# A hybrid-attention layer on one core: sums of output weights formed by DMA in another stage, head outputs loaded one product earlier

## The chip, the cores and the metric

The kernel runs on one core of a Trainium2 chip. Such a core has TensorE (PE, matrix products), VectorE (DVE), ScalarE (ACT) and GpSimd (POOL), and SyncE (SP), which here only starts transfers. Each engine has one queue of instructions and works it off in order; semaphores hold an instruction until what it needs is there. Transfers between the chip's memory and the core's on-chip memory run on 16 DMA engines, which the queues of SP, ACT and POOL feed. The metric is the device time of one execution, in microseconds (us).

## The reference: what is computed

One layer on a sequence of 512 tokens with 16 learned tokens ahead of it, model width 2048, all in 32-bit floats. In short:

```python
u    = rms_norm(h, pre_w)
q_a, ckv, z_a, iq, ik, iw, q_b, k_b, v_b, z_b, g_a, g_b = split(u @ w_in)
# A: index scores pick 128 keys per query; 8 heads attend over a 256-wide latent
o_a  = sparse_attention(q_a, rms_norm(ckv), topk(index(iq, ik, iw)))
# B: 8 heads, difference of two softmaxes, then an RMS norm per head
o_b  = rms_norm((softmax(q1 k1 + bias) - lam * softmax(q2 k2 + bias)) @ v_b) * (1 - lam_init)
y_a  = (o_a * silu(z_a)) @ w_o_a
y_b  = (o_b * silu(z_b)) @ w_o_b
mix  = sigmoid(g_a) * y_a + sigmoid(g_b) * y_b
h    = h + rms_norm(mix @ w_out, post_w)
```

## The kernel before

Every large product is made of three 16-bit products: a float is split into a high and a low 16-bit half after scaling by a power of two. So each block of weights goes the same way. SP loads two halves of 512 KB (tile `raw`, L187 in branch B, L1148 in the gate stage). ACT squares them (`junk`, L123). POOL takes the largest sum over all rows (`rows`, L128). VectorE makes a power of two of it (`exp`, `scale`, L135 to L140). ACT writes the high half (`hi` or `wh`, L169), VectorE the low half (`lo` or `wl`, L170), and PE multiplies both (L289 to L291, L1015). A `raw` buffer is free for the next load when the low half is written.

The stages, by the profiled execution: norm and first projections (to about 100 us), index scores (to 175), branch B (175 to 575), branch A with its query projections (575 to 784), the gates (784 to 1224), the two output projections `w_o` (to 1394) and the product with `w_out` (to the end).

*Branch B* (loop over 8 heads at L882): for each head the projections of q, k and v, each called a unit, of two weight halves. Between the halves the attention of the head before is worked off in steps (`step()`): scores L738 and L739, exponentials L668, their difference `pr` L744, its transposes L675 and the product with V. K is copied out of PE's accumulator by ACT and VectorE at L784 and L785, V by ACT at L900. The bias rows `G` are loaded by SP at L656, and a head's result is stored at L749 and L756.

*Sums of output weights.* The product with `w_out` uses Strassen's scheme, 7 block products in place of 8, and needs four sums of blocks of `w_out`. A chain (`wt_chain`, L254) makes them for one part of 256 KB: two loads by SP (L265) into tiles `wt`; accumulating transfers by POOL's queue (L263), which add another block of memory to the tile; and four stores by SP to a scratch array `wout_t` (L260). There are 16 chains, so 32 loads, 64 additions and 64 stores. A chain goes in six steps with a `yield` between, and later additions wait for the stores of what the tile held before. Before the change two chains belong to each head and advance one step at each `between()` (L878), six times a head, in tiles of the pool `opool`.

*The gates* (`Run`, L1039): the products with the columns of z and g are taken in pairs of blocks, again by Strassen's scheme with 7 products a pair (`Pair.mm`, L1002). Each product is 24 matmuls. `Run.run` walks the list of 154 products, n = 0 to 153, in an order with fixed leads: loads of a pair (blocks A22, A12, A11, A21), squares, scale, sums of the blocks S1 to S4 (L1126) and their split are called so many products ahead. At product 2 of a pair `con.tiles()` took two result tiles and, for pairs of z, called `load_o` for the two heads: it loads a head's output `o` (L1093) and, for branch B's heads, the row factors `rb` (L1096), and multiplies them (L1098). When a pair ends, `gate_o` multiplies by the gate (L1105, L1107) and the result is stored (L1109). The merge gates g store theirs through ACT's queue.

The order on each queue is program order, but for a planner that places the calls; loads, additions and stores of the chains carry `keep_in_program_order`, which holds them in the order of the code against each other.

Of the kernel before, what the change touches and what calls it, by code (L numbers as in the profile page):

```python
# [20 lines left out]
P = 128  # L21
# [6 lines left out]
NH = 8  # L28
# [40 lines left out]
def layer_kernel(ctx, tc, xt_d, xn_d, cols_d, w0_d, wi_d, wkv_d, wo_d, wout_d, lam_d, post_d,  # L69
# [184 lines left out]
    def wt_chain(k, n, tags):  # L254

        t = [opool.tile(HB, F32, tag=tag, name="wt") for tag in tags]
        q = [[wout_d[ci, di, k, :, 512 * n:512 * n + 512] for di in range(2)] for ci in range(2)]

        def put(i, x):
            tc.keep_in_program_order(nc.sync.dma_start(tscr[i][k, :, 512 * n:512 * n + 512], x))  # L260

        def add(x, src):
            tc.keep_in_program_order(nc.gpsimd.dma_start(x, src, accum_op=ALU.add))  # L263
        for i in range(2):
            tc.keep_in_program_order(nc.sync.dma_start(t[i], q[0][i]))  # L265
        yield
        add(t[0], q[0][1])
        add(t[1], q[1][1])
        yield
        put(0, t[0])  # L270
        put(2, t[1])
        yield
        add(t[1], q[0][0])
        yield
        put(1, t[1])
        yield
        add(t[1], q[1][0])
        yield
        put(3, t[1])

    wt_now = []

    def wt_step():
        for g in list(wt_now):
            if next(g, "end") == "end":
                wt_now.remove(g)
# [144 lines left out]
    def side0():  # L431
# [11 lines left out]
        sqi = SC[3][:, :(NB + 1) * 64].rearrange("p (a b) -> p a b", b=64)  # L443
# [30 lines left out]

    def bias_rows():
        oh = [SC[2 + t][:32, :NF // 2] for t in range(2)]
        rb = SC[1][:32, :NIH]
        nc.scalar.dma_start(rb, rb_d)
        pf = lgt()
        for t in range(2):  # L480
            nc.scalar.dma_start(oh[t], oh_d[:, t * NF // 2:(t + 1) * NF // 2])
            nc.tensor.matmul(pf[:NIH, t, :NF // 2], rb, oh[t], start=True, stop=True)
        fsb = pp.tile([NIH, NF], F32, name="fsb")
        nc.vector.tensor_copy(split2(fsb), pf[:NIH, :, :NF // 2])
        nc.scalar.dma_start(fscr.ap(), fsb)
# [16 lines left out]

    piq = [psum(), psum()]
# [374 lines left out]
    def between():  # L878
        wt_step()
        run_topk(TK.pop(0))  # L880

    for h in range(NH):  # L882
        for i in range(2):
            wt_now.append(wt_chain(h, i, [f"o{6 + 4 * (h % 2) + 2 * i + x}" for x in range(2)]))
# [51 lines left out]
    for h in range(NH):  # L936
# [3 lines left out]
        for acc, un in proj_q("qa", h):  # L940
            step()
            wt_step()
# [33 lines left out]
    class Pair:  # L976
# [25 lines left out]
        def mm(self, i):  # L1002
# [14 lines left out]
            v = self.v  # L1017
            if i in (1, 5, 6):
# [20 lines left out]
    class Run:  # L1039
# [23 lines left out]
        def run(self, hooks=None):  # L1063
# [3 lines left out]
            for n, (x, i) in enumerate(self.todo):  # L1067
# [3 lines left out]
                for f in (hooks or {}).get(n - len(self.todo), ()):  # L1071
                    f()
                self.pairs[x].mm(i)

    ogpool = ctx.enter_context(tc.tile_pool(name="ogpool", bufs=1, reuse_waits="tile"))
    zg = ExitStack()
# [14 lines left out]
    def load_o(i):  # L1091
        o = wide("o")
        nc.sync.dma_start(o, oscr[i])  # L1093
        if i >= NH:
            r = wide("rb")
            nc.sync.dma_start(r, bass.AP(tensor=rsq.tensor, offset=rsq.offset + (i - NH) * 512,  # L1096
                                         ap=[[0, P], [1, 512]]))
            nc.vector.tensor_mul(o, o, r)  # L1098
        return o
# [3 lines left out]
    def gate_o(i, o, sz):  # L1103
        if i < NH:
            nc.vector.tensor_mul(sz, sz, o)  # L1105
        else:
            nc.vector.scalar_tensor_tensor(sz, o, gsub, sz, op0=ALU.mult, op1=ALU.mult)  # L1107
# [44 lines left out]
    class Gate:  # L1152
        def __init__(self, func, end, begin=None):
            self.func, self.begin, self.end = func, begin, lambda x: end(x, self)

        def tiles(self):
            self.r = wide("r0"), wide("r1")
            if self.begin is not None:
                self.o = self.begin()
# [341 lines left out]
```

## Time and profile before

| what | before |
|---|---|
| time, median of 3 runs (lowest, highest) | 1552.25 us (1551.74, 1559.52) |
| time of the profiled execution | 1555.86 us |
| its span in the profile | 1554.1 us |
| mean granted clock of TensorE | 0.973 of full |
| busy: PE, VectorE, ACT, POOL | 1438.2, 1104.7, 978.3, 144.3 us |
| moved by DMA | 257.27 MB, 166 GB/s in the mean |
| PE busy in branch B (175 to 575) | 351.4 of 400 us |
| PE busy in the gates (784 to 1224) | 412.3 of 440 us |

A wait in the profile stands for the idle time of an engine ahead of an instruction, with what released it: "PE acc L675 <- DVE pr L744" is PE, idle until VectorE had written the softmax difference. An idle engine costs time only if it ends up delaying PE. Nearly all of the span PE is busy, so what counts is where PE stands still, and where its granted clock is at the lower of its two levels, 1.2 instead of 2.4 GHz.

### The profile page before, as it was taken

The numbers are of one execution on the slowest core, as the hardware profiler recorded it, in microseconds if no ns is written. First come the engines' busy times: TensorE is split into PE (matmuls) and PEld (weight loads), VectorE is DVE, ScalarE is ACT, GpSimd is POOL, SyncE is SP. The second block draws the span as 40 slices with busy tenths as digits, with TensorE's granted clock in tenths as the row PEclk, the third lists the DMA queues.
The fourth block names the chain that finished last, engine by engine and source line by source line (L and its number), as shares of the span: only waits on it lengthen the run. The fifth ranks groups of instructions, "written<-read, shape, count | busy, mean of one in ns | idle before, by whom it ended". The sixth has DMA issues, their size and how long they took to land. (4 is left out here: it accounts for less than half of the span.)

```text
span 1554.1 us, 25269 instructions
## 1 busy us (share of the span) xinstructions
PE 1438.2 (93%) x9475; PEld 1079.5 (69%) x9475; DVE 1104.7 (71%) x2091; ACT 978.3 (63%) x1735; POOL 144.3 (9%) x199
## 2 busy tenths in 40 slices
PE   7799977989898989999999989999999899999997
PEld 7678755766675766665578878888888444458885
DVE  7875756566666677776578887777778455566788
ACT  6365555666565577677677787777778444436555
POOL 3500121212111100000000000000000001000001
PEclk9999998999899999999999999999999999999999
DMA  6383487787777744321545544444344554446774
GB/s 208 124 278 95 126 236 177 202 223 197 180 203 177 210 123 123 116 85 60 191 132 186 178 137 140 144 139 147 122 139 163 174 158 149 150 160 233 240 249 148
DMA packets 104218, 257.27 MB, mean 166 GB/s; under 512 B 12072, under 2 KB 16392, under 8 KB 103968
## 3 DMA queue, kind: packets, MB, share of 16 engines
q1 hardware_dynamic: 86224, 223.86, 44.9%
q0 software_dynamic: 9216, 16.78, 7.0%
q10 hardware_dynamic: 8656, 15.02, 2.7%
q8 instruction: 74, 1.21, 0.3%
q14 instruction: 48, 0.39, 0.1%
HBM read 211.42 MB, written 47.41 MB: 167 GB/s over the span
## 5 line engine op out<-in xcount | busy, mean ns | idle before, releaser
L123 ACT ACTIVATE junk<-raw 128x1024 bf16<-128x1024 f32 x192 | 201.9, 1052 | 139.1 <-DMA raw<-in_wi_dram 122.4
L1015 PEld LDWEIGHTS <-wh 128*128 128x128 f16 x2464 | 242.2, 98 | 61.4 <-issue 32.2
L289 PE MATMUL acc<-u,hi 128*128 128x264 f16 (+1 forms) x832 | 267.8, 322 | 1.0 <-DVE va L836 0.5
L291 PE MATMUL acc<-u,lo 128*128 128x264 f16 (+1 forms) x832 | 266.4, 320 | 1.1 <-DVE lo L170 1.1
L290 PE MATMUL acc<-u,hi 128*128 128x264 f16 (+1 forms) x832 | 266.7, 321 | 0.0
L1015 PE MATMUL acc<-tu,wh 128*128 128x256 f16 x1408 | 237.5, 275 | 27.5 <-DVE r L1024 15.9
L1015 PE MATMUL acc<-tu,wl 128*128 128x256 f16 x704 | 193.7, 275 | 0.0
L169 ACT ACTIVATE hi<-raw,scale 128x1024 f16<-128x1024 f32 x104 | 118.9, 1145 | 116.4 <-PE acc L290 115.1
L1015 PE MATMUL acc<-u,wh 128*128 128x256 f16 x1056 | 175.3, 273 | 0.3 <-ACT q L1019 0.3
L289 PEld LDWEIGHTS <-hi 128*128 128x128 f16 x1088 | 108.2, 99 | 80.6 <-issue 6.0
L291 PEld LDWEIGHTS <-lo 128*128 128x128 f16 x1088 | 108.0, 99 | 78.7 <-DVE lo L170 1.8
L170 DVE SCALAR_TENSOR_TENSOR lo<-raw,scale,hi 128x1024 f16<-128x1024 f32 x104 | 132.7, 1279 | 41.1 <-ACT hi L169 40.6
L290 PEld LDWEIGHTS <-hi 128*128 128x128 f16 x1088 | 108.2, 99 | 73.8 <-issue 1.1
L170 DVE SCALAR_TENSOR_TENSOR wl<-S,scale,wh 128x1024 f16<-128x1024 f32 x88 | 112.7, 1282 | 55.1 <-ACT wh L169 55.0
L128 POOL PARTITION_ALL_REDUCE rows<-ssq x90 | 47.4, 527 | 1066.9 <-ACT junk L123 960.5
L1015 PE MATMUL acc<-u,wl 128*128 128x256 f16 x528 | 143.9, 273 | 0.0
L1015 PEld LDWEIGHTS <-wl 128*128 128x128 f16 x1232 | 121.1, 98 | 14.8
L169 ACT ACTIVATE wh<-S,scale 128x1024 f16<-128x1024 f32 x88 | 100.3, 1141 | 32.1 <-DVE S L1126 32.1
L289 PE MATMUL acc<-og,hi 128*128 128x512 f16 x256 | 97.0, 379 | 0.0
L290 PE MATMUL acc<-og,hi 128*128 128x512 f16 x256 | 97.0, 379 | 0.0
L291 PE MATMUL acc<-og,lo 128*128 128x512 f16 x256 | 97.0, 379 | 0.0
L170 DVE SCALAR_TENSOR_TENSOR wl<-raw,scale,wh 128x1024 f16<-128x1024 f32 x66 | 84.3, 1278 | 10.0 <-ACT wh L169 9.9
(313 smaller groups left out, 2908.1 us busy)
## 6 DMA issues: line engine op xcount, KB each, us to landing
raw<-in_wi_dram SPq DMA_DIRECT2D x172, 512.0 KB, 4.7
wt<-in_wout_dram POOLq DMA_DIRECT2D x64, 256.0 KB, 5.4
wout_t<-wt SPq DMA_DIRECT2D x64, 256.0 KB, 5.1
raw<-in_wo_dram SPq DMA_DIRECT2D x32, 512.0 KB, 3.8
raw<-wout_t SPq DMA_DIRECT2D x32, 512.0 KB, 4.8
raw<-in_wout_dram SPq DMA_DIRECT2D x24, 512.0 KB, 5.6
wt<-in_wout_dram SPq DMA_DIRECT2D x32, 256.0 KB, 5.1
sg<-r ACTq DMA_DIRECT2D x32, 256.0 KB, 2.9
```

The lines of the kernel that those rows point to most:

```text
L123: nc.scalar.activation(j, src, AF.Square, accum_out=dst)
L128: nc.gpsimd.partition_all_reduce(r, ssq, P, bass_isa.ReduceOp.max)
L169: nc.scalar.activation(hi, src, AF.Copy, scale=s)
L170: nc.vector.scalar_tensor_tensor(lo, src, s, hi, op0=ALU.mult, op1=ALU.subtract)
L289: nc.tensor.matmul(out, aH, bH, start=start, stop=False)
L290: nc.tensor.matmul(out, aH, bL, start=False, stop=False)
L291: nc.tensor.matmul(out, aL, bH, start=False, stop=stop)
L1015: nc.tensor.matmul(acc, a[:, k, :], b, start=first and k == 0 and x == 0, stop=last and x == 2, skip_group_check=True)
```

## The change

It has three parts. The chains of weight sums leave branch B and the query loop of branch A and run in the gates: at every odd product n, `wt_step` advances two of them, in two fixed pairs of tiles (og12 to og15 of the pool `ogpool`), and starts the next two when both are through. A chain then takes seven steps, so that 16 chains in two slots take 56 odd products, n = 1 to about 112. Second, a gate pair of z takes its head outputs and row factors at product 1 instead of product 2, in tiles of `ogpool` of their own, and the multiplication of the two moves from the load to the pair's end. Third, the one-hot rows and the bias table are loaded ahead of the loop over the index queries, and the squares of the index keys use a tile of the preparation pool.

```diff
--- before.py
+++ after.py
@@ -253,7 +253,7 @@
 
     def wt_chain(k, n, tags):
 
-        t = [opool.tile(HB, F32, tag=tag, name="wt") for tag in tags]
+        t = [state["ogpool"].tile(HB, F32, tag=tag, name="wt") for tag in tags]
         q = [[wout_d[ci, di, k, :, 512 * n:512 * n + 512] for di in range(2)] for ci in range(2)]
 
         def put(i, x):
@@ -278,12 +278,15 @@
         yield
         put(3, t[1])
 
-    wt_now = []
+    wt_todo = [(k, n) for k in range(8) for n in range(2)]
+    wt_now = [None, None]
 
     def wt_step():
-        for g in list(wt_now):
-            if next(g, "end") == "end":
-                wt_now.remove(g)
+        for x in range(2):
+            if wt_now[x] is None and wt_todo:
+                wt_now[x] = wt_chain(*wt_todo.pop(0), [f"og{12 + 2 * x + y}" for y in range(2)])
+            if wt_now[x] is not None and next(wt_now[x], "end") == "end":
+                wt_now[x] = None
 
     def mm3(out, aH, aL, bH, bL, start, stop):
         nc.tensor.matmul(out, aH, bH, start=start, stop=False)
@@ -440,7 +443,7 @@
         nc.vector.tensor_reduce(st, ikn, AX.X, ALU.add)
         nc.vector.tensor_scalar(st, st, 1.0 / 64, None, op0=ALU.mult)
         nc.vector.tensor_tensor(ikn, ikn, stb, ALU.subtract)
-        sqi = SC[3][:, :(NB + 1) * 64].rearrange("p (a b) -> p a b", b=64)
+        sqi = pp.tile([P, T], F32, tag="sq", name="sqi", bufs=3)[:, :(NB + 1) * 64].rearrange("p (a b) -> p a b", b=64)
         nc.vector.tensor_mul(sqi, ikn, ikn)
         nc.vector.tensor_reduce(st, sqi, AX.X, ALU.add)
         rstd_cols(st, st, 64)
@@ -472,13 +475,17 @@
             nc.scalar.copy(ckH[r], ckv[r])
             nc.vector.tensor_sub(ckL[r], ckv[r], f32(ckH[r]))
 
+    oh = [SC[2 + t][:32, :NF // 2] for t in range(2)]
+    rb = SC[1][:32, :NIH]
+
+    def bias_loads():
+        nc.scalar.dma_start(rb, rb_d)
+        for t in range(2):
+            nc.scalar.dma_start(oh[t], oh_d[:, t * NF // 2:(t + 1) * NF // 2])
+
     def bias_rows():
-        oh = [SC[2 + t][:32, :NF // 2] for t in range(2)]
-        rb = SC[1][:32, :NIH]
-        nc.scalar.dma_start(rb, rb_d)
         pf = lgt()
         for t in range(2):
-            nc.scalar.dma_start(oh[t], oh_d[:, t * NF // 2:(t + 1) * NF // 2])
             nc.tensor.matmul(pf[:NIH, t, :NF // 2], rb, oh[t], start=True, stop=True)
         fsb = pp.tile([NIH, NF], F32, name="fsb")
         nc.vector.tensor_copy(split2(fsb), pf[:NIH, :, :NF // 2])
@@ -500,6 +507,7 @@
         uH[k], uL[k] = u[:, 0], u[:, 1]
         split16(uH[k], uL[k], xT[k], gs[:, k:k + 1])
 
+    bias_loads()
     piq = [psum(), psum()]
     nxt = [first_weights(kp, 3 * P, 5 * P) for kp in range(2)]
     for kp in range(KT // 2):
@@ -876,12 +884,9 @@
                 pending.pop(0)()
 
     def between():
-        wt_step()
         run_topk(TK.pop(0))
 
     for h in range(NH):
-        for i in range(2):
-            wt_now.append(wt_chain(h, i, [f"o{6 + 4 * (h % 2) + 2 * i + x}" for x in range(2)]))
         for acc, un in proj_q("qb", h):
             step(2 if len(pending) == 7 else 1)
             between()
@@ -939,7 +944,6 @@
         step(len(pending) - 2)
         for acc, un in proj_q("qa", h):
             step()
-            wt_step()
         una = wpool.tile([P, 1], F32, tag="una", name="una", bufs=2)
         nc.vector.tensor_scalar(una, un, A_SCALE, None, op0=ALU.mult)
         qh = ap_.tile([P, 512], F32R, tag="q", name="qh", bufs=4)
@@ -1015,6 +1019,8 @@
                     nc.tensor.matmul(acc, a[:, k, :], b, start=first and k == 0 and x == 0,
                                      stop=last and x == 2, skip_group_check=True)
             v = self.v
+            if i == 1:
+                self.con.early()
             if i in (1, 5, 6):
                 nc.scalar.copy(self.q(i), acc)
             elif i == 2:
@@ -1070,9 +1076,12 @@
                 self.prep(n + self.ahead)
                 for f in (hooks or {}).get(n - len(self.todo), ()):
                     f()
+                if n % 2:
+                    wt_step()
                 self.pairs[x].mm(i)
 
     ogpool = ctx.enter_context(tc.tile_pool(name="ogpool", bufs=1, reuse_waits="tile"))
+    state["ogpool"] = ogpool
     zg = ExitStack()
     zp = zg.enter_context(tc.tile_pool(name="zp", bufs=1, reuse_waits="tile"))
 
@@ -1089,22 +1098,22 @@
     nc.sync.dma_start(rsq.rearrange("h (a b) -> (h a) b", b=32), rv)
 
     def load_o(i):
-        o = wide("o")
-        nc.sync.dma_start(o, oscr[i])
+
+        o = [ogpool.tile(HB, F32, tag=f"og{4 * (i % 2) + x}", name="o") for x in range(1 + i // NH)]
+        nc.sync.dma_start(o[0], oscr[i])
         if i >= NH:
-            r = wide("rb")
-            nc.sync.dma_start(r, bass.AP(tensor=rsq.tensor, offset=rsq.offset + (i - NH) * 512,
-                                         ap=[[0, P], [1, 512]]))
-            nc.vector.tensor_mul(o, o, r)
+            nc.sync.dma_start(o[1], bass.AP(tensor=rsq.tensor, offset=rsq.offset + (i - NH) * 512,
+                                            ap=[[0, P], [1, 512]]))
         return o
 
     ogq = zp.tile([P, 2 * NH], F32, name="ogq")
 
     def gate_o(i, o, sz):
         if i < NH:
-            nc.vector.tensor_mul(sz, sz, o)
+            nc.vector.tensor_mul(sz, sz, o[0])
         else:
-            nc.vector.scalar_tensor_tensor(sz, o, gsub, sz, op0=ALU.mult, op1=ALU.mult)
+            nc.vector.tensor_mul(o[0], o[0], o[1])
+            nc.vector.scalar_tensor_tensor(sz, o[0], gsub, sz, op0=ALU.mult, op1=ALU.mult)
         squares(sz, ogq[:, i:i + 1])
         nc.sync.dma_start(gscr[i], sz)
 
@@ -1153,10 +1162,12 @@
         def __init__(self, func, end, begin=None):
             self.func, self.begin, self.end = func, begin, lambda x: end(x, self)
 
+        def early(self):
+            if self.begin is not None:
+                self.o = self.begin()
+
         def tiles(self):
             self.r = wide("r0"), wide("r1")
-            if self.begin is not None:
-                self.o = self.begin()
 
     pairs = []
     for i in list(range(NDIRECT, NH, 2)) + list(range(NH, 2 * NH, 2)):
```

SP's queue in one head of branch B, before (`wout_t<-wt` is a store of a sum, `wt<-in_wout_dram` a load of a block to be summed):

```order
L260 DMA wout_t<-wt 128x512 x2
L265 DMA wt<-in_wout_dram 128x512 x4
L187 DMA raw<-in_wi_dram 128x1024
L749 DMA o_f<-ob 128x512
L187 DMA raw<-in_wi_dram 128x1024
L756 DMA o_sumsq<-row 1x512
L260 DMA wout_t<-wt 128x512 x4
L187 DMA raw<-in_wi_dram 128x1024 x2
L260 DMA wout_t<-wt 128x512 x2
L656 DMA G<-bias_rows 128x528
L187 DMA raw<-in_wi_dram 128x1024 x2
```

and after:

```order
L187 DMA raw<-in_wi_dram 128x1024 x3
L757 DMA o_f<-ob 128x512
L187 DMA raw<-in_wi_dram 128x1024
L764 DMA o_sumsq<-row 1x512
L187 DMA raw<-in_wi_dram 128x1024 x2
L664 DMA G<-bias_rows 128x528
```

The stores and loads of the sums are gone, and the loads of weights stand next to the head's own few transfers.

SP's queue in two merge-gate pairs of the gates, before (four loads a pair, in the order A22, A12, A11, A21):

```order
L1148 DMA raw_10400<-in_wi_dram 128x1024
L1148 DMA raw_10398<-in_wi_dram 128x1024
L1148 DMA raw_10394<-in_wi_dram 128x1024
L1148 DMA raw_10396<-in_wi_dram 128x1024
L1148 DMA raw_10647<-in_wi_dram 128x1024
L1148 DMA raw_10645<-in_wi_dram 128x1024
L1148 DMA raw_10641<-in_wi_dram 128x1024
L1148 DMA raw_10643<-in_wi_dram 128x1024
```

and after, from the load of A22 of a pair on:

```order
L1157 DMA raw_10564<-in_wi_dram 128x1024
L260 DMA wout_t1<-wt_10450 128x512
L260 DMA wout_t3<-wt_10451 128x512
L260 DMA wout_t1<-wt_10454 128x512
L260 DMA wout_t3<-wt_10455 128x512
L1157 DMA raw_10562<-in_wi_dram 128x1024
L260 DMA wout_t2<-wt_10451 128x512
L1157 DMA raw_10558<-in_wi_dram 128x1024
L1157 DMA raw_10560<-in_wi_dram 128x1024
L260 DMA wout_t2<-wt_10455 128x512
L1157 DMA raw_10819<-in_wi_dram 128x1024
L260 DMA wout_t4<-wt_10451 128x512
```

Between the four loads of such a pair now stand five stores, and one more behind them; the next pair's A22 has the last stores of the two chains behind it.

POOL's queue from the first additions on, before (`rows<-ssq` is the all-reduce of one unit's squares):

```order
L128 ISA rows<-ssq 128x2
L263 DMA wt<-in_wout_dram 128x512 x4
L128 ISA rows<-ssq 128x2
L263 DMA wt<-in_wout_dram 128x512 x2
L128 ISA rows<-ssq 128x2
L263 DMA wt<-in_wout_dram 128x512 x2
L128 ISA rows<-ssq 128x2 x2
L263 DMA wt<-in_wout_dram 128x512 x6
L128 ISA rows<-ssq 128x2
L263 DMA wt<-in_wout_dram 128x512
```

and after, from the same place in branch B:

```order
L128 ISA rows<-ssq 128x2 x34
L128 ISA rows<-ssq 128x4 x2
L263 DMA wt<-in_wout_dram 128x512 x6
L128 ISA rows<-ssq 128x4
L263 DMA wt<-in_wout_dram 128x512 x2
L128 ISA rows<-ssq 128x4
L263 DMA wt<-in_wout_dram 128x512 x6
L128 ISA rows<-ssq 128x4
L263 DMA wt<-in_wout_dram 128x512 x2
L128 ISA rows<-ssq 128x4
```

The all-reduces of branch B stand in a row, and those of the gates (128x4) have the additions between them, six and two in turn.

## Rows read from the trace of the kernel before

**Rows 1.** The page's first line, the profiled execution:
```profile
span 1554.1 us, 25269 instructions
```

**Rows 2.** Window of branch B; busy us (instructions) per engine, clock, DMA share, GB/s:
```profile
175.00:575.00 400.00, 351.41 (x2408) 259.80 (x2407) 262.19 (x727) 241.43 (x469) 65.11 (x90) 0.93 0.74 193
```

**Rows 3.** Waits of PE in 175:575; awaited releaser: us in total, times, longest:
```profile
PE acc L675 <- DVE pr L744: 33.4, 7, 6.6
PE acc L716 <- ACT vt L900: 7.8, 2, 3.9
PE s L738 <- DVE mx L665: 4.5, 1, 4.5
```

**Rows 4.** Windows over nine stretches of half clock in branch B, their sum:
```profile
sum 54.70, PE 40.39 PEld 31.93 DVE 40.84 ACT 27.16 POOL 2.93; mean PE 4.49 PEld 3.55 DVE 4.54 ACT 3.02 POOL 0.33
```

**Rows 5.** Timeline of ACT, head 5; start, us, line, tiles, idle before and its releaser:
```profile
379.44 1.06 ACT L123 ACTIVATE junk<-raw 128x1024 bf16<-128x1024 f32 x1 [4.77 <-DMA raw<-in_wi_dram]
...
395.44 1.06 ACT L123 ACTIVATE junk<-raw 128x1024 bf16<-128x1024 f32 x1 [1.39 <-DMA raw<-in_wi_dram]
...
398.89 1.06 ACT L123 ACTIVATE junk<-raw 128x1024 bf16<-128x1024 f32 x1 [2.30 <-DMA raw<-in_wi_dram]
```

**Rows 6.** Timeline of SP's queue in the same stretch:
```profile
375.02 8.60 SPq L260 DMA_DIRECT2D wout_t<-wt  x4
391.12 3.20 SPq L187 DMA_DIRECT2D raw<-in_wi_dram  x2
```

**Rows 7.** Waits of all engines in 175:575:
```profile
POOL rows L128 <- DMA wout_t<-wt: 47.1, 4, 12.2
...
ACT junk L123 <- DMA raw<-in_wi_dram: 79.4, 30, 5.8
```

**Rows 8.** Timelines of SP and ACT ahead of the weight sums, 134:139:
```profile
134.36 21.94 SPq L187 DMA_DIRECT2D raw<-in_wi_dram  x4
...
138.11 1.06 ACT L123 ACTIVATE junk<-raw 128x1024 bf16<-128x1024 f32 x1 [2.46 <-DMA raw<-in_wi_dram]
```

**Rows 9.** DMA queues and issues in 175:575; packets, MB, share; KB each, us to landing:
```profile
q1 hardware_dynamic: 24206, 57.77, 44.6%
q0 software_dynamic: 9216, 16.78, 27.1%
...
raw<-in_wi_dram SPq DMA_DIRECT2D x52, 512.0 KB, 5.0
...
wout_t<-wt SPq DMA_DIRECT2D x64, 256.0 KB, 5.1
```

**Rows 10.** Window of gate products 1 to about 112:
```profile
786.00:1088.00 302.00, 288.45 (x2609) 255.69 (x2608) 241.88 (x284) 229.08 (x355) 8.32 (x16) 0.99 0.47 152
```

**Rows 11.** Timelines of POOL and SP, first two pairs of weight-sum chains:
```profile
197.26 3.86 POOL L263 DMA_DIRECT2D wt<-in_wout_dram  x4 [0.25 <-DVE exp L135]
...
231.64 0.89 POOL L263 DMA_DIRECT2D wt<-in_wout_dram  x1 [2.46 <-DMA wt<-in_wout_dram]
...
201.68 5.67 SPq L260 DMA_DIRECT2D wout_t<-wt  x4
...
238.82 4.79 SPq L260 DMA_DIRECT2D wout_t<-wt  x4
```

**Rows 12.** Timelines of SP and ACT, two merge-gate pairs:
```profile
931.42 0.97 SPq L1148 DMA_DIRECT2D raw<-in_wi_dram  x2
...
935.24 1.06 ACT L123 ACTIVATE junk<-raw 128x1024 bf16<-128x1024 f32 x1 [1.26 <-DMA raw<-in_wi_dram]
...
954.38 1.06 ACT L123 ACTIVATE junk<-raw 128x1024 bf16<-128x1024 f32 x1 [1.69 <-DMA raw<-in_wi_dram]
```

**Rows 13.** Waits in the gate stage: PE 784:930, then DVE 784:1224:
```profile
PE acc L1015 <- ACT q L1019: 8.1, 6, 2.2
...
DVE o L1098 <- DMA rb<-o_rstd: 10.1, 7, 2.5
```

**Rows 14.** Timeline of PE in the first stage:
```profile
82.04 0.71 PE L482 MATMUL lg<-sc,sc 32*16 32x328 f32 x2 [1.78 <-DMA sc<-in_oh_dram]
```

## The prediction, made before the changed kernel was run

> **What bounds the kernel now.** I read the page first: the profiled execution spans 1554.1 us [rows 1], and its own time of 1555.9 us is 1.8 us more than that, start and end. The median shown, 1552.25 us, is 3.6 us below this execution. I sum changes against the execution and take them off the median, since none of them depends on which execution it is. TensorE (PE) sets the time: busy 1438 of 1554 us by the page. So only idle PE, and PE at half clock, can be given back. The windows by stage come next. Branch B, where the weight sums run today, has PE busy 351.4 of 400 us at a mean granted clock of 0.93, with the 16 DMA engines at 0.74 [rows 2]. The other stretch that the change touches, gate products 1 to 112, has PE busy 288.5 of 302 us, clock 0.99, DMA at 0.47 [rows 10]. So 48.6 us are idle in the first and 13.5 us in the second.
>
> The waits of PE name three stalls in branch B: seven at L675, the transposes of the softmax rows, 33.4 us; two at L716, 7.8 us; one at L738, 4.5 us [rows 3]. After each the clock falls to its lower level (1.2 of 2.4 GHz) for a while: nine such stretches, 54.7 us long with PE busy for 40.4 of them [rows 4]. What PE did there would take half as long at full clock: 20.2 us. So the most that branch B can give is 45.7 + 20.2 = 66 us.
>
> Who is late? Ahead of a typical L675 stall ACT waits 1.39 and 2.30 us for the two halves of the next weight block, with the K copies (L784) behind them in its queue [rows 5]. Just before, it waited 4.77 us for another half, while SP was held for 8.60 us on four stores of sums [rows 5, 6]. Over the branch ACT waits 79.4 us for such halves, and four all-reduces of the squares on POOL stood 47.1 us behind additions that waited for a store [rows 7]. At the branch's start, before the first sum, a half is squared 3.75 us after its issue (134.36 to 138.11) [rows 8]; in head 5 that time is 4.3 us for the first half (391.12 to 395.44) [rows 5, 6].
>
> **The change, part by part.** *Sums leave branch B.* 32 loads, 64 additions and 64 stores go. The additions' queue is q0, 27.1% of 400 us, or 108 us of all 16 engines. The rest is 96 x 0.262 MB = 25.2 MB; at q1's rate, 44.6% of 400 us for 57.77 MB, that is 78 us [rows 9]. DMA demand falls from 296 to 110 us of 400.
> The seven L675 stalls have two bounds. Above: all 33.4 us. Below: only the latency goes; if each stall shrinks by the 5.0 - 3.75 us between a half's median landing in this branch and its time before the sums [rows 8, 9], that is 7 x 1.25 = 9 us. I take 19. In four heads, like head 5, the halves before are late too, so that the whole wait of 1.39 + 2.30 = 3.7 us should nearly go (4 x 3.5); in three PE itself releases the buffer, and only some 1.6 us go. What is late next is the softmax chain itself (K copies on ACT and VectorE, scores, exponentials), and it keeps about 2 us a head. The L738 stall goes whole, 4.5 us: VectorE waited there for an all-reduce queued behind an addition [rows 3, 7]. Of L716's 7.8 us, where ACT copies V behind a square that waits for its block, I take half, 3.5. Of the 20.2 us of half clock [rows 4] I let 11 go, a little less than in proportion to the stalls, of which 27 of 45.7 us go. Branch B: 19 + 4.5 + 3.5 + 11 = 38 us, between 17 (9 + 4.5 + 3.5) and 66.
>
> *Sums enter the gate stage.* Each pair of chains takes seven steps, one at every odd product, so 14 products, two gate pairs. A pair lasts 19.14 us (935.24 to 954.38) [rows 12], so one loop has 38.3 us and there are eight. Two workings of the cost:
> (i) Latency. The first loop in branch B, with no raw load ahead of its stores, ran from its first addition to that of the next in 231.64 - 197.26 = 34.4 us; there the next chain had other tiles, here it waits for the last store, 5.1 us [rows 9, 11]. That makes 39.5 us, 1.2 us too long: 8 x 1.2 = 10 us. In the second loop four additions took until their last store issued 12.0 us (231.64 to 243.61), in the first 10.1 us (197.26 to 207.35) [rows 11]. With 1.9 us more on each of the three addition steps a loop is 45.2 us: 8 x 6.9 = 55 us. What queues behind it: SP is one queue in program order, and in every second pair the load of A12 stands behind four stores and that of A11 behind one more, each of which waits for an addition. Nothing is spare there: the A11 load is issued at 931.42 and squared at 935.24, with ACT already waiting 1.26 us [rows 12].
> (ii) Bandwidth. The stretch uses 0.47 x 302 = 142 us of the 16 engines [rows 10]; 186 us come to it. 142 + 186 = 328 us in 302: 26 us too many, if shares add up to 1. They do add: q1 and q0 with the small queues are the 0.74 of rows 2.
> The Trainium skill says the same of the mechanism in "DMA: Bandwidth & Descriptors", section "Issuing engines are not separate DMA queues": transfers started by SP, ACT and POOL end up on the same 16 engines and interleave. The sum of shares above agrees; if q0 had engines of its own, only (i) would count, and the forecast would be 15 us lower.
> The two are not added, since a saturated engine is what makes a loop long. I take 25 us, next to (ii) and inside 10 to 55.
> The additions also stand between the all-reduces on POOL. I cost that at nothing: the scale made of an all-reduce is asked for one product later, 19.14 / 7 = 2.7 us, and feeds weights that are built two to three products ahead of PE; if the additions hold it for longer than that, it comes on top.
>
> *Head outputs and row factors at product 1, multiply at the gate's end.* VectorE's seven waits for the row factors, 10.1 us, go [rows 13]. PE's part is at most the 8.1 us that it waited for ACT's copies there [rows 13]; I take 5. The multiply itself (eight in all) only moves. The new tiles are free long before, so product 1 gains no wait. Bounds 0 and 8.
>
> *One-hot rows early, and a prep-pool tile for the indexer squares.* The 1.78 us that PE waits at L482 go [rows 14]. In the first stage the additions of squares on POOL now stand ahead of the all-reduce; I bound what that does by -4 and +4 us and take 0. Together -2.
>
> Sum: -38 + 25 - 5 - 2 = -20 us: 1536 us for an execution like the profiled one, **1532 us** by the median.
>
> **Rivals.** *A. Slower: the gate stage runs at the pace of the sums.* If loads and the three addition steps each take 1.9 us more than in the first loop, a loop is 39.5 + 7.6 = 47.1 us, and eight loops cost 8 x 8.8 = 70 us: 1552 - 45 + 70 = 1577 us. It decides from a loop of 43.9 us on, where 8 x 5.6 equals the 45 us gained elsewhere. For it: the demand of 328 us in 302, and A11 without slack. Against: early gate pairs fetch much further ahead, and the transfers of the merge gates are few between two pairs.
> *B. Branch B hardly moves*, because the L675 stalls are the softmax chain's own. Then 17 us are gained and no clock: -17 + 25 - 7 = +1, 1553 us. For it: VectorE and ACT are busy 262 and 241 of 400 us [rows 2], so no engine rests long. Against: ACT's 79.4 us.
> *C. The gate stage hides the sums*: loops at 38.3 us or less, cost 5: -38 + 5 - 7 = -40, 1512 us. For it: half of its DMA time is free today.
> *D. Branch B gives nearly all its 66 us*: -66 + 25 - 7 = -48, 1504 us; with C 1484.
>
> **How the numbers follow.** My forecast 0.46 (1516 to 1546, with gate costs of 10 to 40), A 0.17, B 0.12, C 0.19, D 0.06. A measurement can tell 0.5%, 8 us, from no change. Faster (below 1544.5): 0.43 + 0.02 (B) + 0.19 + 0.06 = 0.70. Same: 0.03 + 0.08 (B) = 0.11. Slower: 0.17 + 0.02 (B) = 0.19. The range from 1500 to 1567 leaves out about half of A and the lower part of D and C.
>
> **What would show it.** Branch B: DMA near 0.3, the wait at L675 between 10 and 20 us in total, none at L738, clock above 0.96, additions' waits gone from POOL. Gate stage: DMA share above 0.85 in products 1 to 112, first additions of two loops some 40 us apart, PE idle there near 13.5 + 20 us, ACT waiting for A11 longer than 1.26 us in merge-gate pairs. VectorE's row-factor waits gone. The forecast is wrong if L675 keeps over 25 us, or if loops pass 44 us.

## The result, and the profile after

The change made the kernel slower: 1605.53 us in the median (1603.97 to 1608.10, 4 runs) against 1551.99 us for the kernel before, a ratio of 1.0345 with a 95% interval of 1.0295 to 1.0395. The forecast was 1532 us, so direction and size are both wrong. The profiled execution took 1605.2 us in its span.

Where it went shows when the start of the gates' first product is read from both traces, and then every 28th product (four gate pairs; 24 matmuls make a product):

| kernel | gates start | n 0-28 | 28-56 | 56-84 | 84-112 | 112-154 | gates in all |
|---|---|---|---|---|---|---|---|
| before | 784.2 | 77.7 | 81.8 | 75.1 | 76.3 | 129.0 | 439.9 |
| after | 740.3 | 87.5 | 101.8 | 110.6 | 106.1 | 128.8 | 534.7 |

The gates start 43.9 us earlier, and last 94.8 us longer, all of it in the products with sums; what follows takes 330 us in both. (Twelve kernels here, the changed one among them, have the same code ahead of the gates, and their gates start between 737.9 and 746.4 us; differences of a few us in the start tell nothing.) These rows are the windows and waits of the changed kernel, with the columns of [rows 2] and [rows 3]; the second window goes from the first product to product 112:

```profile
175.00:575.00 400.00, 377.10 (x2656) 276.67 (x2655) 295.74 (x826) 273.00 (x541) 10.80 (x29) 0.99 0.33 99
740.00:1146.00 406.00, 316.76 (x2689) 272.58 (x2688) 248.48 (x290) 236.07 (x367) 63.80 (x81) 0.90 0.78 216
```

```profile
PE acc L683 <- DVE pr L752: 17.0, 7, 6.2
...
PE acc L724 <- ACT vt L905: 1.3, 1, 1.3
```

Branch B is what was forecast: against [rows 2, 3] PE is idle for 23 instead of 49 us, the clock is 0.99 instead of 0.93, the transposes wait 17.0 instead of 33.4 us. The gates answer to [rows 10], whose 302 us end at product 109; the same 112 products before, and the ten stretches of the changed kernel at half clock, in sum:

```profile
784.20:1095.10 310.90, 297.35 (x2690) 263.69 (x2689) 248.66 (x293) 236.84 (x367) 8.74 (x17) 0.99 0.46 149
```

```profile
sum 78.50, PE 40.83 PEld 28.81 DVE 34.41 ACT 49.60 POOL 4.63; mean PE 4.08 PEld 2.88 DVE 3.44 ACT 4.96 POOL 0.46
```

PE is idle for 89 us in 406 where it was idle for 13.5 us in 311, which is 76 of the 95 us. The other 19 are the clock: PE is busy for 40.8 us at 1.2 GHz, where before it was for 3.4 us, and half of the difference is lost. These are PE's waits there, and the longest of ACT's:

```profile
PE acc L1019 <- ACT q L1025: 76.8, 14, 11.9
PE acc L1019 <- DVE r L1030: 11.0, 6, 5.7
```

```profile
ACT junk L123 <- DMA raw<-in_wi_dram: 96.0, 11, 14.6
```

PE waits for ACT to copy a product out, and ACT stands in front of a square whose weights have not come. One merge-gate pair shows the waits, queue by queue (timelines of POOL, SP, ACT and PE after the change; start, length, instruction, idle time before it and its releaser; they answer to [rows 12]):

```profile
926.96 0.37 POOL L128 PARTITION_ALL_REDUCE rows<-ssq  x1 [17.08 <-ACT junk L123]
927.44 3.58 POOL L263 DMA_DIRECT2D wt<-in_wout_dram  x4
939.92 0.86 POOL L263 DMA_DIRECT2D wt<-in_wout_dram  x1 [8.90 <-DMA wout_t<-wt]
...
958.37 0.37 POOL L128 PARTITION_ALL_REDUCE rows<-ssq  x1 [15.88 <-ACT junk L123]
958.82 1.79 POOL L263 DMA_DIRECT2D wt<-in_wout_dram  x2
```

```profile
932.79 6.11 SPq L260 DMA_DIRECT2D wout_t<-wt  x4
939.00 0.38 SPq L1157 DMA_DIRECT2D raw<-in_wi_dram  x1
945.81 0.32 SPq L260 DMA_DIRECT2D wout_t<-wt  x1
946.22 0.88 SPq L1157 DMA_DIRECT2D raw<-in_wi_dram  x2
```

```profile
951.51 1.06 ACT L123 ACTIVATE junk<-raw 128x1024 bf16<-128x1024 f32 x1 [13.96 <-DMA raw<-in_wi_dram]
```

```profile
952.98 0.58 PE L1019 MATMUL acc<-tu,wh 128*128 128x256 f16 x2 [10.17 <-ACT q L1025]
```

Follow it round. The first four additions go out at 927.44, right behind an all-reduce that had waited 17 us for its squares. The stores wait for them until 932.79 to 938.9, the load of A12 stands behind the stores; the next addition waits for a store, the next store for it (945.81), and A11 and A21 stand behind that one (946.22). They are squared from 951.51 on, 14 us after ACT was ready. Only then come the squares for the next all-reduce (958.37), and the last additions stood behind that. From all-reduce to all-reduce it is 31.4 us, where a pair took 19.1 us. How much of this the waits make, and how much the traffic itself, the experiments tell.

### The profile page after: what moved, and what is told of

The parts are those of the page before. It is cut to its first block, busy times and chain, and to the rows that moved or that the text cites. A ratio compares the mean times of both kernels' runs of the same rounds, so it can differ in the third digit from the quotient of the medians.

```text
span 1605.2 us, 25304 instructions
## 1 busy us (share of the span) xinstructions
PE 1442.2 (90%) x9475; PEld 1078.4 (67%) x9475; DVE 1104.8 (69%) x2091; ACT 978.7 (61%) x1735; POOL 146.7 (9%) x199
## 5 line engine op out<-in xcount | busy, mean ns | idle before, releaser
L1019 PE MATMUL acc<-tu,wh 128*128 128x256 f16 x1408 | 254.5, 287 | 101.5 <-ACT q L1025 78.8
L1019 PEld LDWEIGHTS <-wh 128*128 128x128 f16 x2464 | 248.2, 101 | 142.2 <-issue 104.8
L292 PE MATMUL acc<-u,hi 128*128 128x264 f16 (+1 forms) x832 | 263.4, 317 | 0.7 <-DVE va L844 0.5
L294 PE MATMUL acc<-u,lo 128*128 128x264 f16 (+1 forms) x832 | 263.1, 316 | 0.0
L293 PE MATMUL acc<-u,hi 128*128 128x264 f16 (+1 forms) x832 | 263.1, 316 | 0.0
L1019 PE MATMUL acc<-tu,wl 128*128 128x256 f16 x704 | 201.9, 287 | 0.0
L128 POOL PARTITION_ALL_REDUCE rows<-ssq x90 | 42.7, 474 | 1084.2 <-ACT junk L123 1052.9
```

The costliest lines, as they stand in the source:

```text
L128: nc.gpsimd.partition_all_reduce(r, ssq, P, bass_isa.ReduceOp.max)
L292: nc.tensor.matmul(out, aH, bH, start=start, stop=False)
L293: nc.tensor.matmul(out, aH, bL, start=False, stop=False)
L294: nc.tensor.matmul(out, aL, bH, start=False, stop=stop)
L1019: nc.tensor.matmul(acc, a[:, k, :], b, start=first and k == 0 and x == 0, stop=last and x == 2, skip_group_check=True)
```

## The experiments

Theory L (lock) is this loop of waits. Its rival B is bandwidth: [rows 10] and the sums' traffic made 328 us of DMA time in 302. A later theory J says that the weight loads of the gates come just in time, so that any burst of transfers in front of them costs PE. The table has the times of all runs, with the ratio to the kernel before and its 95% interval, and the stretches from the traces. The kernel before was timed beside each lot of runs, with medians from 1546 to 1553 us, so a difference of a few us between two lots is trusted only where the lengths of the gates show it too:

| run | us | ratio (interval) | gates start | n 0-56 | 56-112 | gates |
|---|---|---|---|---|---|---|
| e1 four slots | 1591.1 | 1.025 (1.020-1.030) | 740.8 | 193.0 | 197.7 | 515.6 |
| e2 no sums | 1504.0 | 0.969 (0.962-0.975) | 738.1 | 153.3 | 154.2 | 434.0 |
| e3 free stores | 1576.0 | 1.015 (1.008-1.022) | 741.8 | 185.7 | 192.4 | 504.0 |
| e4 sums in B | 1549.2 | 0.998 (0.996-1.001) | 779.5 | 155.5 | 153.0 | 435.1 |
| e5 no waits | 1576.8 | 1.017 (1.013-1.022) | 743.9 | 177.0 | 197.9 | 500.8 |
| e6 half | 1560.2 | 1.006 (1.004-1.009) | 760.8 | 172.7 | 171.5 | 471.0 |
| e7 third | 1597.9 | 1.030 (1.026-1.034) | 753.2 | 176.3 | 195.3 | 514.4 |
| e8 phase | 1615.2 | 1.042 (1.037-1.047) | 746.4 | 197.3 | 215.9 | 539.9 |
| e9 ring | 1597.9 | 1.031 (1.025-1.037) | 737.9 | 186.5 | 215.5 | 527.2 |
| e12 plain | 1576.9 | 1.018 (1.012-1.024) | 739.7 | 175.8 | 198.7 | 503.6 |
| e13 GpSimd, B | 1533.6 | 0.990 (0.985-0.995) | 764.6 | 154.9 | 154.0 | 436.2 |
| e14 GpSimd, gates | 1614.4 | 1.042 (1.036-1.048) | 738.7 | 224.9 | 192.5 | 543.0 |
| e15 no waits, plain | 1553.2 | 1.004 (1.001-1.006) | 738.7 | 172.4 | 181.8 | 481.2 |
| e16 no waits, no additions | 1516.8 | 0.981 (0.978-0.983) | 738.5 | 159.3 | 158.1 | 444.0 |
| e17 VectorE, B | 1524.1 | 0.986 (0.983-0.988) | 761.4 | 154.5 | 152.7 | 432.5 |
| e18 ring, early | 1590.7 | 1.029 (1.027-1.031) | 737.9 | 187.0 | 210.5 | 520.6 |
| e19 VectorE, gates | 1538.2 | 0.992 (0.989-0.994) | 742.4 | 170.0 | 169.3 | 465.7 |

**What the sums cost, e2.** `wt_step()` taken out of `Run.run` (the product with `w_out` then reads plain blocks, a line not shown):

```diff
-                if n % 2:
-                    wt_step()
```

> The changed kernel without any sums of weights (the product with w_out reads plain blocks in their place, same bytes). It gives what the sums cost in the gates. Both theories: branch B as in the changed kernel, the gates at 440 us less the 5 us of part two, so 1500 us within 5; L and B differ only on the cause of the 100 us between.

1504.0 us: 101 us below the changed kernel, all in the gates, which take 434.0 us. PE's wait at the transposes of branch B stays at 16.7 us, so those are not the sums'. That they are the softmax chain's own is not shown: ACT still waits 42 us in all for halves of weights there. This run is the ground for all others.

**Parts two and three alone, e4.** `wt_step()` and its old chains back in `between()` and the query loop:

```diff
     def between():
+        wt_step()
         run_topk(TK.pop(0))
...
-                if n % 2:
-                    wt_step()
```

> Parts two and three of the change alone: sums stay in branch B and the query loop as before. Both theories: 5 us from the gates and 2 us from the first stage, 1545 us (1540 to 1550).

1549.2 us, a ratio whose interval holds 1: not told apart from the kernel before. The trace gives the gates 435.1 us, 4.8 less than before, where 5 were forecast, and e2 agrees with 434.0.

**Twice the time for each wait, e1.** Four chains in flight, two advanced at a time:

```diff
-    wt_now = [None, None]
+    wt_now = [None] * 4
...
-        for x in range(2):
+        for x in (2 * ph, 2 * ph + 1):
...
-                    wt_step()
+                    wt_step(n // 2 % 2)
```

> Four chains of sums in flight in place of two (tiles og8 to og15), each advanced at every fourth product, so that bytes per product stay and each wait has twice the time. Theory L (lock): in the changed kernel SP's loads stand behind stores that wait for additions, and POOL's additions behind all-reduces that wait for squares of those loads; twice the time opens the loop, the merge-gate pairs return from 31 us to about 20 us, and the time is 1535 to 1550 us. Theory B (bandwidth): the 16 DMA engines are the bound, bytes per product are the same, and the time stays at 1590 us or more.

1591.1 us: L's number missed, B's held by 1 us. SP still stood 100 us at stores, where it had stood 135 us:

```profile
SPq L260 <- DMA wt<-in_wout_dram: 100.2, 34, 6.6
```

The additions are still behind the all-reduces, and the merge-gate pairs take 24 to 26 us (102.4 and 95.3 us for four), not 20: doubling the steps did not open the loop. A miss for L in the form that I had given it.

**Stores that wait for nothing, e3.** `put` reads one fixed tile:

```diff
-nc.sync.dma_start(tscr[i][k, :, 512 * n:512 * n + 512], x)
+nc.sync.dma_start(tscr[i][k, :, 512 * n:512 * n + 512], state["fix"])
```

> The changed kernel with every store of a sum read from one fixed tile, so that no store waits for an addition and no addition for a store; same loads, additions, stores and bytes, what is stored is not the sum. L: SP never holds a load back, only the traffic is left, some 27 us over no sums at all: 1520 to 1540 us. B: nearly nothing changes, 1590 us or more.

1576.0 us, between the two: 30 us go, 72 stay. But loads of blocks still waited for additions, so e5 takes all waits away: additions go to tiles of their own.

```diff
-        add(t[0], q[0][1])
-        add(t[1], q[1][1])
+        add(d[0], q[0][1])
+        add(d[1], q[1][1])
...
-        add(t[1], q[0][0])
+        add(d[2], q[0][0])
```

> The changed kernel with the same loads, additions and stores of sums at the same products, but none waits for another: additions go to tiles of their own, stores read one fixed tile, and each tile comes round again only some 20 to 38 us later. What is stored is not the sum. It gives the price of the traffic alone, between no sums (1504 us) and the changed kernel (1605 us). L: 27 us over no sums, 1530 us (1520 to 1545). B: 1575 us or more, as in the run with free stores.

1576.8 us, the same. So waits between the sums' transfers make 29 us, and the traffic with no wait in it 73 us. L alone is refuted. The trace of e5 shows how (POOL, SP, ACT, PE):

```profile
948.42 0.42 POOL L128 PARTITION_ALL_REDUCE rows<-ssq  x1 [21.71 <-ACT junk L123]
948.71 1.80 POOL L263 DMA_DIRECT2D wd<-in_wout_dram  x2
969.90 0.42 POOL L128 PARTITION_ALL_REDUCE rows<-ssq  x1 [19.39 <-ACT junk L123]
970.20 5.37 POOL L263 DMA_DIRECT2D wd<-in_wout_dram  x6
997.74 0.41 POOL L128 PARTITION_ALL_REDUCE rows<-ssq  x1 [22.17 <-ACT junk L123]
```

```profile
979.23 1.82 SPq L1166 DMA_DIRECT2D raw<-in_wi_dram  x2
```

```profile
990.88 1.06 ACT L123 ACTIVATE junk<-raw 128x1024 bf16<-128x1024 f32 x1 [10.38 <-DMA raw<-in_wi_dram]
```

```profile
992.34 0.59 PE L1019 MATMUL acc<-tu,wh 128*128 128x256 f16 x2 [7.89 <-ACT q L1025]
```

Six additions leave at once when the all-reduce ahead of them is through. The load issued at 979.23 is squared at 990.88, 11.7 us later, where the same load took 3.8 us in [rows 12]; between 970.2 and 979.2 SP had also issued six stores and another load. The Trainium skill's "DMA: Bandwidth & Descriptors" (section "Issuing engines are not separate DMA queues") has transfers of all issuers interleave on the same 16 engines, and this row agrees. Two and six additions leave in turn, so the rows give a price for each: from all-reduce to all-reduce a merge-gate pair takes 21.5 us behind two (22.1 in the mean of three) and 27.8 us behind six (27.6 in the mean of four), where it takes 19.9 us in e16 (below), which has no additions. That is 1.1 and 1.3 us for each addition: six at once cost hardly more apiece than two.

B has the mean rate decide. In products 0 to 56 of e5 the engines are busy 0.94 of the time, so there they may well be the bound; in products 56 to 112 they are at 0.71:

```profile
914.00:1112.00 198.00, 155.91 (x1330) 134.30 (x1330) 120.11 (x136) 114.87 (x172) 31.00 (x40) 0.91 0.71 208
744.00:914.00 170.00, 149.55 (x1297) 129.56 (x1295) 125.12 (x150) 115.55 (x187) 31.87 (x40) 0.96 0.94 274
```

The next two runs have less traffic per product:

**Less traffic, e6 and e7.** Half of the chains in branch B and a step every fourth product (e6); two chains in head 0 and a step every third (e7). The lines that keep chains in branch B are not shown:

```diff
-                if n % 2:
+                if n % 4 == 1:      # e7: n % 3 == 0
```

> Half of the 16 chains stay in branch B (one a head instead of two), the other half run in the gates, two at a time, a step at every fourth product instead of every second, so half the traffic and twice the time for a step. L and B both expect the gates near 434 us plus 5 to 15; branch B gives back some 25 of its 44 us: 1530 us (1515 to 1545).

> Two chains stay in head 0 of branch B, fourteen run in the gates with a step at every third product instead of every second: two thirds of the traffic per product, and a loop of 57 us where the changed kernel's took 40 to 56 us. L: the loop fits, so the stalls of the merge gates nearly go: gates at 450 us, 1525 us (1515 to 1540). B: traffic falls by a third, 1560 us or more.

e6: 1560.2 us, gates 471.0, 37 us over none for half the traffic, and its gates start at 760.8 us, 22.7 us later than in e2: that much the chains left in branch B cost. Both theories had 1545 us at most and missed. e7: 1597.9 us, where L missed by 58 us, and B had only a lower bound, 1560 us. Its gates start at 753.2 us, 15 later than in e2, and take 80 us more than with no sums. By chain run in the gates that is 5.7 us in e7 (14 chains), 4.6 in e6 (8) and 6.3 in the changed kernel (16): at two thirds of the rate a chain costs nearly its full price. In products 56 to 112 of e7 PE is 41 us later than in e2, with the engines at 0.64, so no mean rate explains it:

```profile
929.00:1125.00 196.00, 162.25 (x1352) 138.59 (x1351) 119.97 (x137) 113.11 (x168) 22.95 (x31) 0.92 0.64 182
```

**Phase, e8.** First step at product 3:

```diff
-                if n % 2:
+                if n >= 3 and n % 2 == 1:
```

> The changed kernel with its first step at product 3 instead of product 1; all else follows two products later, so that POOL has four additions between each two all-reduces instead of six and two in turn. L: what stands behind what changes, so the time moves by 10 us or more, either way. B: same bytes at the same rate, within 5 us of 1605 us.

1615.2 us, 10 us more, but 6 of them stand ahead of the gates (746.4 against 740.3 us), where nothing was changed. The gates take 539.9 instead of 534.7 us. In total that is just short of L's 10 us, in the gates just over B's 5: this run does not tell the two apart.

**More lead, e9 and e18.** Seven weight buffers (not shown), and with e18 loads called four products earlier (shown):

```diff
-                    self.at.setdefault(self.begin[x - 1] - 2, []).append(pairs[x].fetch)
+                    self.at.setdefault(max(self.begin[x - 1] - 2 - 4, -2), []).append(pairs[x].fetch)
```

> The changed kernel with seven weight buffers in the gates instead of six (A11, A21 and A12 go round one ring), so that a load may start one load earlier. J (the loads of the merge gates come just in time, and whatever stands before them in a queue or in the DMA engines delays PE): the extra lead takes 10 to 30 us off, 1575 to 1595 us. L alone: loads wait on SP behind stores, not for buffers, so within 5 us of 1605 us.

> The changed kernel with seven weight buffers and each gate pair's loads called four products earlier, so that in SP's queue they stand ahead of more of the stores. J: lead is what is missing, 1570 to 1590 us (1598 with the buffers alone). L: loads still stand behind the first stores of their pair, 1590 us or more.

1597.9 and 1590.7 us: 8 and 15 us less than the changed kernel, and the gates are 7.5 and 14 us shorter. Both are just short of what J expected; e9 is outside L's 5 us, e18 just inside L's range (1590 us or more). Lead helps a little, and decides nothing between L and J.

**Plain transfers in place of additions, e12, and without waits, e15; no additions, e16.**

```diff
-nc.gpsimd.dma_start(x, src, accum_op=ALU.add)
+nc.gpsimd.dma_start(x, src)
```

> The changed kernel with the 64 additions as plain transfers from the same queue into the same tiles (nothing is added, so what is stored is not the sum): same order, waits and bytes, but some 0.7 instead of 1.7 us of all 16 engines each. J: bursts of six additions shrink from 10 to 4 us, the just-in-time loads land sooner: 1550 to 1575 us. L: the loop gets shorter by about 2 us per addition step only: 1580 to 1595 us.

> The kernel without waits between the sums' transfers, with its 64 additions as plain transfers as well (what is stored is not the sum). J (bursts of additions in the DMA engines ahead of just-in-time loads): each burst of six shrinks from 10 to 4 us, so the 7 to 8 us stalls of every second merge-gate pair nearly go: 1535 to 1555 us. If the number of transfers or their issue by GpSimd is what counts, 1570 us or more.

> The same without any additions: only the 32 loads and 64 stores of the sums run in the gates, without waits (what is stored is not the sum). J: 1515 to 1530 us, since what is left are short plain transfers spread over SP's queue; if loads and stores on SP's queue are what delays the weight loads, 1550 us or more.

1576.9, 1553.2 and 1516.8 us, as J expected but for 2 us at e12, which lies between J's range and L's. With e5 and the changed kernel that is a square: additions cost 24 us more than plain transfers without waits (1577 to 1553) and 29 us with them (1606 to 1577); the waits cost 29 us with additions and 24 us with plain transfers. The 64 plain transfers from POOL's queue cost 36 us more than none (1553 to 1517), loads and stores of the sums 13 us (1517 to 1504; 10 us by the length of the gates). PE's waits from 900 to 1100 us, of e5, e15 and e16 in turn:

```profile
PE acc L1019 <- ACT q L1025: 38.1, 8, 7.9
```

```profile
PE acc L1019 <- ACT q L1025: 19.7, 7, 4.3
```

```profile
PE acc L1019 <- ACT q L1025: 1.6, 3, 0.8
```

The stall goes with what POOL's queue sends behind an all-reduce. e16 moves 25 MB more than e2 in the gates, in 96 transfers from SP's queue, and costs 13 us. The mean rate does not part the two: these are products 56 to 112 of e15 and of e16,

```profile
911.00:1093.00 182.00, 157.09 (x1349) 135.64 (x1347) 119.74 (x135) 113.29 (x169) 19.40 (x41) 0.94 0.64 226
```

```profile
898.00:1056.00 158.00, 148.29 (x1346) 131.35 (x1344) 118.89 (x132) 111.93 (x168) 2.98 (x8) 1.00 0.60 207
```

at 0.64 and 0.60, and they are 28 and 4 us longer than in e2.

**Sums without accumulating transfers, e13, e14, e17, e19.** Four plain loads, four additions on the chip, four stores, in branch B (e13, e17) or in the gates (e14, e19), on GpSimd or VectorE. The loads all go by SP's queue, so POOL's sends nothing for the sums any more. e17 and e19 also move one addition of squares in the first stage (`sqc`) from GpSimd to VectorE:

```diff
+        nc.gpsimd.tensor_add(d, b, d)     # e17, e19: nc.vector
+        nc.gpsimd.tensor_add(b, a, b)
...
+        put(2, d)
+        put(0, b)
+        nc.gpsimd.tensor_add(a, a, d)
...
+        put(1, a)
+        nc.gpsimd.tensor_add(c, c, a)
...
+        put(3, c)
```

> Sums in branch B as before, parts two and three kept, but no accumulating transfers: each chain loads four blocks with plain transfers, GpSimd adds on the chip (64 additions of 128x512), and no addition waits for a store. DMA demand in branch B falls from 296 to about 215 of 400 us. J and L: most of the late loads go, 1515 to 1530 us. If GpSimd's additions slow VectorE or hold the all-reduces, 1540 us or more.

> The changed kernel with the same on-chip sums in the gates (four plain loads, four additions on GpSimd and four stores a chain, tiles og8 to og15, steps at the same products). Traffic in the gates falls by 80 us of the 16 engines and the loop has no transfer in it but loads. J: 1540 to 1565 us, since loads of weights still stand behind stores on SP that wait for additions. B (bandwidth alone): 1520 us.

> On-chip sums in branch B as in the run with GpSimd's additions (1534 us), but added by VectorE: 64 additions of some 0.7 us, 45 us more work on VectorE in 400, none on GpSimd, whose all-reduces then stand alone. Branch B should lose some 10 us of its 26 us of sums: 1520 to 1530 us. If VectorE's queue delays the softmax chain instead, 1535 us or more.

> Sums in the gates at the products of the changed kernel, but made of four plain loads, four additions on VectorE and four stores a chain. If accumulating transfers are what made the gates slow: 1504 us without sums, 13 us for loads and stores, and 10 to 25 us for 45 us more work on VectorE, which is busy for some 80% there: 1525 to 1545 us. If the place is what counts (stores ahead of just-in-time loads on SP, whoever adds): 1570 us or more.

GpSimd in branch B 1533.6 us, 4 us above J's range; in the gates 1614.4 us, which J missed by 50 us and B by 94. There POOL itself is late (its waits in the gates, e14):

```profile
POOL rows L128 <- issue: 50.6, 7, 9.0
```

Seven times an all-reduce behind an addition of GpSimd starts some 7 us (5.9 to 9.0) after anything that it waits for. The stores wait for POOL, and the loads for the stores. VectorE in branch B gives 1524.1 us and in the gates 1538.2 us, both as expected. So with additions on VectorE the two places differ by 14 us, and the same place, the gates, differs by 67 us between accumulating transfers and VectorE. In branch B that difference is 25 us (e4 to e17), and with accumulating transfers the two places differ by 56 us (e4 to the changed kernel). So neither the place nor the way of adding is the cause alone: the change was slow because it brought accumulating transfers into the gates. e17 beats both kernels, with a ratio of 0.986 to the kernel before. What it pays for the sums against e2 is some 23 us ahead of the gates. Half of that is the clock: seven stretches at half clock with PE busy for 26.8 us, where e2 has one with 4.8, cost 11 us more. The other half stands at the transposes in branch B, 27.5 against 16.7 us; VectorE does the softmax there too, which I take for the reason:

```profile
PE acc L681 <- DVE pr L750: 27.5, 7, 7.2
```

## Why the prediction was wrong

*Sums leave branch B: right.* 38 us and 2 us were forecast, and the gates start 43.9 us earlier. L675 lost 16.4 us (19 forecast), and the 2 us a head that stay are not the sums': e2 has them too. L738 went whole, L716 lost 6.5 us (3.5 forecast). One stretch of half clock is left, with PE busy for 5.1 us where it was 40.4, so the clock gave back 17 to 18 us, more than the 11 allowed for. Rival B, stalls that stay, is out.

*Part two: right*, 5 us by the traces of e2 and e4, too small for e4's time to tell; in the changed kernel itself VectorE waits 13.1 us for head outputs again. *Part three:* the wait at L482 is gone, but the index scores begin at 100.14 instead of 100.70 us, and other traces with the same code begin them at 98.4 to 100.6; the 2 us forecast are not shown.

*Sums enter the gate stage: wrong.* The term was 25 us and measured 101 us (e2), above its upper bound of 55. Of the 101 us the waits make 29 and the traffic without them 73 (e5). Four steps of it failed; the first two are those of the waits.
First, the all-reduces. I cost the additions between them "at nothing", and asked only whether an addition could hold an all-reduce. It is the other way round: an addition stands behind an all-reduce, which waits up to 22 us for squares (17.1 us in the rows above), and then up to four of them (six in e5) leave at once. This order was there in POOL's queue to be read.
Second, the latency was summed from branch B, where stores and additions had no such wait in front. The first additions of two loops in the merge gates are 56.0 us apart (927.44 above, and 983.46 below), not 39.5 or 45.2: two pairs of 31.4 and 24.6 us, where the budget was 38.3:

```profile
983.46 3.58 POOL L263 DMA_DIRECT2D wt<-in_wout_dram  x4
```

Third, and largest, working (ii) took a mean rate as the price of traffic: only demand above 1 was to cost anything. In products 56 to 112 of e5 PE is 44 us late with the engines at some 0.71: what costs is a transfer ahead of a load with no slack, 1.1 to 1.3 us for each addition. (The window of (ii) ended at product 109; to 112 it has 311 us, and the excess is 21 us, not 26. That changes little.) The figure for slack was on the table (3.8 us from issue to square, ACT already waiting [rows 12]) and was used only for stores, not for transfers that share the engines.
Fourth, the term had no clock in it. Branch B's stalls were priced with their half clock, those that the sums make in the gates without; it cost 19 us there.
Rival A was right in direction, and its chance was put at 0.17. Its mechanism, SP's queue at the pace of the sums, was there too, with loops of 56 us in the merge gates instead of 47; but without any such wait (e5) 73 of the 101 us remain, which its sum does not have.

What stays open: why 64 plain transfers from POOL's queue cost 36 us (e15) where 96 from SP's cost 13 (e16). That they leave together is not the reason that the rows give: in e15 a pair takes 24.0 us behind six of them and 21.7 behind two, 0.7 and 0.9 us for each. That they leave at a moment when the pair's loads are due fits, but no run sent the same transfers at another moment of the pair, or from SP's queue. (e19 sends 128 from SP's queue, and its gates are 32 us longer than those of e2, VectorE's additions included.) And e7, whose steps are longest, has not been taken apart.

## What to carry to other kernels

A transfer moved to a stage with free bandwidth is not free there: look at what it stands behind in its own queue, and at how long a load of that stage may be late. Where loads come just in time, put nothing ahead of them that waits, and price each transfer that leaves right ahead of them, whatever the mean load; here it cost 0.7 to 1.3 us apiece. Where stalls are added, add the half clock behind them. If a sum can be made on an engine from plain loads, price that before an accumulating transfer; here it was worth 67 us at the same place.

## What the runs showed of the hardware

GpSimd's all-reduce directly after one of its elementwise additions started 5.9 to 9.0 us late with nothing else to wait for, seven times (e14). The other way round it was as late: in e13 six additions behind an all-reduce waited 42.4 us in all, up to 7.5, with no cause in the profile. The reason was not tested. The same addition of 128x512 floats took 1.40 us on GpSimd (e13) and 0.68 us on VectorE (e17); the columns are count, busy us, mean ns of one and idle time ahead:

```profile
L275 POOL TENSOR_TENSOR wt<-wt 128x512 f32<-128x512 f32 x16 | 22.3, 1398 | 1.1
```

```profile
L275 DVE TENSOR_TENSOR wt<-wt 128x512 f32<-128x512 f32 x16 | 10.8, 682 | 0.1
```

A load of 512 KB that takes 3.8 us in the quiet gates took 11.7 us behind six additions, six stores and another load (e5).
